# Output projection from rounded parts, with the gate on the result, more work buffers and another order of issue

## The chip, the core and the metric

The kernel runs on one core of one Trainium2 chip. A core has a matrix engine (TensorE, PE in the profile, with its weight loads listed as PEld), a vector engine (VectorE, DVE), an activation engine (ScalarE, ACT), a general engine (GpSimd, POOL) and an engine that here only issues transfers (SyncE, SP). Each takes its own instructions in the order in which they stand, and waits on semaphores for the others. Work data lie in an on-chip memory of 128 partitions (SBUF), matrix results in a second one (PSUM). Transfers are issued on the queue of SP or of POOL.

The metric is the device time of one execution in microseconds (us), as the median of several runs. Less is better.

## What is computed

One hybrid decoder layer for 1024 tokens of width 1024, float32 in and out. Normalised and modulated input goes through one projection into the inputs of two mixers: sparse attention with three branches (8 heads of 64), and a diagonal state-space model (S5). Each mixer's 512 columns are multiplied by a SiLU path, and both go through one output projection; its result is gated per column and added to the input:

```python
shift, scale, gate = jnp.split(silu(c) @ w_ada + b_ada, 3, axis=-1)
h = rms_norm(x, norm_g) * (1 + scale[:, None, :]) + shift[:, None, :]
proj = h @ w_in                                  # q, k/v of three branches, gate paths, S5 input
attn = nsa_attention(...) * silu(z_a)            # (1, 1024, 512)
ssm = glu(gelu(s5_mixer(u, ...))) * silu(z_s)    # (1, 1024, 512)
mix = jnp.concatenate([attn, ssm], axis=-1) @ w_out
return x + gate[:, None, :] * mix
```

The change concerns the last two lines above: the product with `w_out` (1024 x 1024), the gate, and the sum with x.

## The kernel before

Tokens are worked in 8 tiles of 128 (index i). The program is a list of some 500 named items. A table, `ORD`, gives the order in which the items are written; each item puts its instructions into the queues of the engines that it uses. What an engine does next is therefore set by `ORD` and by the way in which the items' instructions are merged per engine. A second table, `FLG`, says for single steps on which engine they run: "d" DVE, "p" POOL, "a" ACT, "t" a transfer that adds to what is there.

Stages, in the order in which they mainly run:

- Start. x is loaded in two halves (`xl_`), squared (`sq`), scaled (`xsc`) and transposed (`xb`). The modulation is computed from 24 chunks of `w_ada` (`ma`, `mb`, `mod`). `h_chunk` makes the modulated input h as two F32R tiles, a rounded part `hhi` and a rest `hlo`. The input projection (`kva`, `kvb`, `qa`, `qb`, `u`, `c_mms`) multiplies h with weights that are split in the same way (`split_w`: ACT copies the weight into an F32R tile, DVE or POOL subtracts that from the weight): rounded by rounded, rounded by rest, rest by rounded, three F32R matmuls into one sum. In the profile these are L325 to L327 and L346.
- S5 (`prep`, `tab`, `mats`, `scan`, `out`, four groups s). `mats` makes small matrices on PE (`pk`, `pw`) from tables that DVE and POOL prepare; `scan` makes `pvv` on PE, then a chain of ACT and DVE steps (`zw`, `z`), then PE takes `z` in the products `py` (L847, L848). Keys are normalised and rotated (`kpan`; the rotation writes `kr`) and transposed on PE (`kpat`, `pkt`, L474).
- Attention. For each of 8 tiles and 8 heads: `ha` (scores `S` on PE, L1147; the maximum on DVE, L1164; exp on ACT into `pp`, L1180), `hs`, `hb` (ACT scales into f16 `hl`, L1199), `hc` (DVE makes the f16 rest, L143; SP transposes `hl` into `PT` by transfer), `ub` (PE multiplies `PT` with the values V, L1240). Tiles run 0 to 3, then 7, 6, 5, 4. `z` pieces, items of the input projection, are spread between the heads.
- Output. `glu` writes the S5 half of the mix into `ps`. `wout(half, k)` loads 128 rows of `w_out` and multiplies them with the gate row, twice 128x512 on DVE. `ssm_out(i)` (`so`) multiplies the S5 half of tile i with weights of half 1 in float32 (L1041, `po<-wo,ps`) and DVE adds x from PSUM. `attn_trans(i)` (`at`) transposes the attention result and multiplies it with its SiLU path (`za`); `attn_out(i, n)` (`ao`) multiplies it with weights of half 0 (L1041, `po<-wo,za`) and `out_half` adds the S5 result and issues the store. The last tile, 4, does this in `last_out`, in two groups of heads.

One product here is one 128x128 block of the mix times one 128x512 block of `w_out`: 8 tiles x 2 halves of the columns x 4 blocks x 2 mixers are 128 products. A float32 product stands in the profile as two matmul records.

Work tiles come from pools of fixed slots: `w4` tiles of 4 KB per partition (`N4` = 16 slots), `w2` of 2 KB (`N2` = 12), `f2` of 2 KB in the late part (`F2` = 6). The default memory for the descriptors of POOL's transfers takes 16 KB of each partition.

Of the kernel before, what the change touches and what calls it, by code (L numbers as in the profile page):

```python
# [32 lines left out]
mats1 kpb0 kpb1 kpbn0 u1 u2 cU3 kpbn1 mod0 tab1 qaw0 xl1 u3 out0 prep2 scan1 cVC tab2 cmpk out1 qaw1 qaw2 cmpv kpbt0
xl2 mod1 mod2 mats2 qaw3 qa0 qaw4 hidk qaw5 cok kpbt1 qa1 mod3 qaw6 mod4 qa2 qa3 qaw7 prep3 mod5 tab3 mod6 qa4 qa5 qa6
qa7 qp0 qp1 qpn0 qpn1 qb0 tq qs0 hidv gw xl3 qs1 qw0 scan2 qr0 cz0 mats3 scan3 qb1 cov scalev qb2 qb3 cmpK qb4 gates
qt00 qb5 qb6 qb7 mod7 z0_0 modf cz2 cz1 z0_1 out2 qpb0 qpb1 qpbn0 g2 qt01 qpbn1 qsb1 z0_2 z0_3 ca0 z0_4 z0_5 z0_6 z1_0
z0_7 out3 kt ha00 ha01 qsb0 hs01 hb00 hc00 qw1 qr1 z1_1 z1_2 ct0 z1_3 ha02 ha03 hs03 hb01 hb02 z1_4 z1_5 cz3 ha04 hc01
hc02 z1_6 ha05 z1_7 hb03 hs05 hb04 hb05 yp00 z2_0 qt10 hc03 hc04 hc05 ha06 ha07 z2_1 z2_2 z2_3 z2_4 hs07 hb06 ha10 ca1
hb07 cz4 ha11 z2_5 ub00 qt11 ub01 hs11 hb10 hc06 hc07 z2_6 z2_7 hc10 ub02 qw2 ha12 yp01 ub03 hb11 qr2 ha13 ct1 z3_0
z3_1 z3_2 ub04 ub05 hs13 z3_3 z3_4 ha14 z3_5 ub06 ub07 cz5 hb12 hc11 hc12 ha15 hb13 z3_6 hc13 z3_7 hs15 hb14 qt20 z4_0  # L40
ha16 ha17 z4_1 ub10 ub11 hs17 hb15 hc14 hb16 ub12 yp02 z4_2 z4_3 ha20 ca2 hb17 hc15 hc16 qt21 z4_4 z4_5 cz6 z4_6 ub13
ha21 hs21 ha22 z4_7 yp03 hb20 hc17 ub14 yp10 ub15 hb21 z5_0 z5_1 z5_2 z5_3 qw3 qr3 ha23 hs23 hc20 hc21 hb22 ub16 cz7
# [1542 lines left out]
```

## Time and profile before

| | |
|---|---|
| median of 3 runs | 716.23 us (716.12 to 720.16) |
| profiled execution, its own time | 714.4 us |
| profiled execution, span of the core | 712.6 us |
| mean granted clock of TensorE in it | 0.983 |
| instructions in it | 12253 |

The profile is one execution on the chip. Its parts are the busy time of each engine, groups of equal instructions with mean duration and the idle time ahead of them, waits (who waited for whom), a timeline of single instructions, stretches of the span with the busy time of each engine in them, and the chain of work that ended last. A row of the timeline gives start, duration, engine, line, operation, what is written and from what, shape, count, and in square brackets how long the engine had been idle and what released it. Line numbers are those of the kernel before; in the changed kernel they are higher by 5 or more.

### The profile page before, as it was taken

The page shows a single profiled execution, that of the slowest core. Times are in us where ns is not written, and L with a number is a line of the kernel's source. Part 1 is how long each engine was busy: PE and PEld are TensorE (multiplying, and loading weights), DVE is VectorE, ACT ScalarE, POOL GpSimd, SP SyncE. Part 2 cuts the span into 40 slices and gives each one's busy share as a digit, 9 for nine tenths or more (in the row PEclk, how much of TensorE's full clock was granted, in tenths as well). Part 3 has the DMA queues.
Part 4 walks back from the last instruction along what each step waited for, and adds up shares of the span by engine and source line. Part 5 has one row for each costly group of instructions (what it writes and reads, how often), then busy time and mean ns, then how long its engine had stood idle before and what let it go on. Part 6 is the DMA issues. An engine that isn't in the chain of part 4 may idle for free. (4 is left out here: it accounts for less than half of the span.)

```text
span 712.6 us, 12253 instructions
## 1 busy us (share of the span) xinstructions
PE 640.2 (90%) x4534; PEld 469.4 (66%) x4534; DVE 541.3 (76%) x1077; ACT 359.2 (50%) x700; POOL 135.9 (19%) x152
## 2 busy tenths in 40 slices
PE   3399978599999999998998999998899899999997
PEld 1267767488788887886776776655566665665554
DVE  5989998678837889756686786988878786777561
ACT  4376205623551154446676775735575662755340
POOL 0150219247111020650201101120002011010000
PEclk9989998889999999999999999999999999999999
DMA  8963023046476723293556649769989795879674
GB/s 328 378 205 82 1 59 119 18 126 158 92 232 174 215 79 106 76 260 79 163 141 162 168 134 244 204 149 238 257 193 187 178 206 120 175 171 204 148 187 92
DMA packets 209470, 115.95 MB, mean 163 GB/s; under 512 B 159041, under 2 KB 188481, under 8 KB 209410
## 3 DMA queue, kind: packets, MB, share of 16 engines
q1 hardware_dynamic: 206146, 109.91, 60.3%
q0 software_dynamic: 3264, 5.26, 3.0%
q8 instruction: 36, 0.59, 0.4%
q14 instruction: 24, 0.20, 0.1%
HBM read 58.10 MB, written 18.61 MB: 108 GB/s over the span
## 5 line engine op out<-in xcount | busy, mean ns | idle before, releaser
L1180 ACT ACTIVATE pp<-S,st 128x640 f32<-128x640 f32 (+7 forms) x128 | 88.5, 697 | 75.1 <-DVE st L1164 53.8
L143 DVE SCALAR_TENSOR_TENSOR hl<-pp,st,hl 128x640 f16<-128x640 f32 (+7 forms) x128 | 94.9, 777 | 13.2 <-ACT hl L1199 12.7
L1199 ACT ACTIVATE hl<-pp,st 128x640 f16<-128x640 f32 (+7 forms) x128 | 85.7, 729 | 18.2 <-DVE hl L143 5.7
L346 PE MATMUL pcp<-hhi,wh 128*128 128x512 f32 x208 | 85.3, 410 | 2.8 <-DVE ql L143 2.1
L346 PE MATMUL pcp<-hhi,wl 128*128 128x512 f32 x208 | 82.9, 398 | 0.0
L346 PE MATMUL pcp<-hlo,wh 128*128 128x512 f32 x208 | 82.7, 398 | 0.0
L1164 DVE TENSOR_REDUCE st<-S 128x1 f32<-128x1024 f32 (+3 forms) x64 | 57.4, 917 | 12.2 <-PE S L1147 11.5
L325 PE MATMUL ptp<-wsp,hhi 128*128 128x512 f32 x128 | 52.3, 412 | 12.1 <-ACT hhi L291 12.1
L1147 PE MATMUL S<-kT,qh 128*128 128x512 f32 (+3 forms) x192 | 58.7, 363 | 1.7 <-ACT pp L1180 1.4
L1240 PEld LDWEIGHTS <-PT 128*128 128x128 f16 x1584 | 54.7, 98 | 7.4 <-issue 7.1
L1041 PE MATMUL po<-wo,za 128*128 128x512 f32 x128 | 58.6, 601 | 1.0 <-DVE za L143 0.6
L1240 PE MATMUL po<-V,PT 128*128 128x64 f16 x1584 | 58.7, 193 | 0.0
L1041 PE MATMUL po<-wo,ps 128*128 128x512 f32 x128 | 57.7, 599 | 0.4 <-DVE Sc L146 0.3
L1147 PE MATMUL S<-kT,ql 128*128 128x512 f32 (+3 forms) x192 | 53.6, 339 | 0.0
L327 PE MATMUL ptp<-wsp,hlo 128*128 128x512 f32 x128 | 51.7, 406 | 1.7 <-POOL hlo L146 1.3
L326 PE MATMUL ptp<-wsp,hhi 128*128 128x512 f32 x128 | 52.5, 410 | 0.1
L146 POOL TENSOR_TENSOR Sc<-Sc,lc 128x512 f32<-128x512 f32 x8 | 9.1, 1138 | 222.6 <-DVE lc L146 203.3
L1147 PEld LDWEIGHTS S<-kT,qh 128*128 128x128 f32 x192 | 32.6, 190 | 23.0 <-issue 18.1
L346 PEld LDWEIGHTS pcp<-hhi,wh 128*128 128x128 f32 x208 | 39.6, 190 | 11.3 <-issue 2.5
L346 PEld LDWEIGHTS pcp<-hlo,wh 128*128 128x128 f32 x208 | 39.2, 189 | 9.2
L346 PEld LDWEIGHTS pcp<-hhi,wl 128*128 128x128 f32 x208 | 39.3, 189 | 8.0
L1041 PEld LDWEIGHTS po<-wo,ps 128*128 128x128 f32 x128 | 23.4, 190 | 26.5 <-issue 24.4
(317 smaller groups left out, 1303.7 us busy)
## 6 DMA issues: line engine op xcount, KB each, us to landing
wada<-in_w_adaT_dram SPq DMA_DIRECT2D x24, 512.0 KB, 5.9
wr<-in_w_in_dram SPq DMA_DIRECT2D x14, 512.0 KB, 4.2
x<-in_x_dram SPq DMA_DIRECT2D x8, 512.0 KB, 5.8
wo<-in_w_out_dram SPq DMA_DIRECT2D x8, 512.0 KB, 5.3
xo<-in_x_dram SPq DMA_DIRECT2D x16, 256.0 KB, 4.1
out_dram<-ps SPq DMA_DIRECT2D x16, 256.0 KB, 2.4
wraw<-in_w_in_dram SPq DMA_DIRECT2D x15, 256.0 KB, 3.5
ud<-U SPq DMA_DIRECT2D x4, 512.0 KB, 3.1
```

What stands on the lines that cost most here:

```text
L143: dve.scalar_tensor_tensor(out=o, in0=a, scalar=s, in1=b, op0=o0, op1=o1, **kw)
L146: e.tensor_tensor(out=o, in0=a, in1=b, op=op)
L325: pe.matmul(p, H(k)[:, tsl], w[:, 0, :], start=k == 0, stop=False)
L326: pe.matmul(p, H(k)[:, tsl], w[:, 1, :], start=False, stop=False)
L327: pe.matmul(p, H(k, True)[:, tsl], w[:, 0, :], start=False, stop=k == 7)
L346: pe.matmul(p[:], w[:, k, :], H(k, l)[:, halves(half)], start=(k == 0 and w is hi and not l), stop=(k == 7 and l))
L1041: pe.matmul(p, a(k), M["wo", half, k][:, halves(n)], start=k == 0, stop=k == 3)
L1147: pe.matmul(R[:, c0:c1], w, x, start=bank not in opened, stop=False, skip_group_check=True)
L1164: dve.tensor_reduce(out=st[br], in_=us[br][0][:, :W], axis=AX.X, op=OP.max, negate=True)
L1180: act.activation(pp[:, :W], R[:, :W], AF.Exp, bias=st[br], accum_out=st4[:, 1, 2 * (h % 2) + br:2 * (h % 2) + br + 1])
L1199: act.activation(hl[:, :W], pp[:, :W], AF.Copy, scale=st[br])
L1240: pe.matmul(o, p, v, start=first, stop=end, skip_group_check=True)
```

## The change

- The weights of the output projection are loaded into a work tile (`wor`) and split into a rounded F32R tile and a rest, ACT copying and DVE subtracting (`wo..` is "d" throughout). The product with the gate row on the weights is gone.
- The mix of a tile is split as well (`parts`): ACT copies it into an F32R tile `oh`, DVE or POOL subtracts into `ol`. Of the 15 whole tiles, 9 subtractions are on POOL (`so0`, `so2`, `so7`, `at0` to `at3`, `at5`, `at6`) and 6 on DVE; the last tile's two halves are on DVE.
- A product becomes three F32R matmuls: 384 in place of 128 float32 products.
- The gate multiplies the result: `ssm_out` writes sum x 0.125 x gate into `ps` and then adds x, `out_half` writes sum x gate into a new tile `o` and then adds `ps`. That is two DVE steps of 128x512 where one stood. For tile 2 x is added by a transfer on POOL's queue.
- A weight needs two tiles now, so half 1 takes the slots that half 0 had. `wo0` therefore waits for all `so`, and `wo1` for all `glu`.
- The memory for descriptors is 2 KB, not 16; the 14 KB make three more `w4` slots and one more `w2`.
- `ORD` is another order; some `FLG` of the earlier stages move (three more parts of h by POOL transfer, two squares from DVE to ACT, one S5 step and one weight split from POOL to DVE, one weight split to POOL).

```diff
 ORD = """
-xl_0 sc1 sq1 sc0 sq2 sq3 sq0 rstd0 xsc0 xb10 ma0 ma5 mb0 xl_1 sq5 sq4 xb00 kvaw0 sq7 lb mg mc0 sq6 rstd1 h00 kva0 xsc1
+sc1 sc0 lb pu xl_0 sq0 sq2 sq1 sq3 ma7 mb4 ma0 rstd0 mb0 kvaw0 ma5 xl_1 xsc0 sq5 xb10 sq4 xb00 sq6 sq7 mg mc0 h00 mb2
...
-N4, N2, F2 = 16, 12, 6
+N4, N2, F2 = 19, 13, 6
+SCRATCH = 2048
...
     def wout(half, k):
-        w = p4([128, 1024], F32, "wo") if half else s4([128, 1024], F32, "wo", 0)
+        w = p4([128, 1024], F32R, "wo"), s4([128, 1024], F32R, "wo", 0)
         r0 = 512 * half + 128 * k
-        dma(w[:], t["w_out"][r0:r0 + 128, :], "o")
-        for n in range(2):
-            stt(w[:, halves(n)], w[:, halves(n)], 0.125 if half else 1.0, M["gate"][:, halves(n)], OP.mult, OP.mult)
+        on = FLG.get(f"wo{half}{k}", "d")
+        if on == "t":
+            fetch_w(w[0][:], w[1][:], t["w_out"][r0:r0 + 128, :])
+        else:
+            raw = w4([128, 1024], F32, "wor")
+            dma(raw[:], t["w_out"][r0:r0 + 128, :], "o")
+            split_w(w[0][:], w[1][:], raw[:], {"p": pool, "d": dve}[on])
         M["wo", half, k] = w
-    def outproj(p, a, half, n, ks=range(4)):
-        for k in ks:
-            pe.matmul(p, a(k), M["wo", half, k][:, halves(n)], start=k == 0, stop=k == 3)
+    def outproj(p, a, half, n, ks=range(4)):
+        for k in ks:
+            w = M["wo", half, k]
+            for m, (x, y) in enumerate(((0, 0), (0, 1), (1, 0))):
+                pe.matmul(p, a[x][:, k, :], w[y][:, halves(n)], start=k == 0 and m == 0, stop=k == 3 and m == 2)
+    def parts(a, tile_, on):
+        hi, lo = tile_([128, 4, 128], F32R, "oh"), tile_([128, 4, 128], F32R, "ol")
+        f = lambda x: x[:].rearrange("p a b -> p (a b)")
+        act.copy(f(hi), a)
+        tt(on, f(lo), a, f32(f(hi)), OP.subtract)
+        return hi, lo
     def ssm_out(i):
         ps = M["ps"]
-        sums = []
+        a = parts(ps[:, i, 0:512], f2, {"p": pool, "d": dve}[FLG.get(f"so{i}", "p")])
         for n in range(2):
-            xo = f2([128, 512], F32, "xo")
-            dma(xo[:], xr[:, i, halves(n)], "i")
             p = pmm("po")
-            outproj(p[:], lambda k: ps[:, i, 128 * k:128 * k + 128], 1, n)
-            sums.append((p, xo))
-        for n, (p, xo) in enumerate(sums):
-            tt(dve, ps[:, i, halves(n)], p[:], xo[:], OP.add)
+            outproj(p[:], a, 1, n)
+            stt(ps[:, i, halves(n)], p[:], 0.125, M["gate"][:, halves(n)], OP.mult, OP.mult)
+            on = FLG.get(f"xa{i}", "d")
+            if on != "t":
+                xo = f2([128, 512], F32, "xo")
+                dma(xo[:], xr[:, i, halves(n)], "i")
+                tt({"p": pool, "d": dve}[on], ps[:, i, halves(n)], ps[:, i, halves(n)], xo[:], OP.add)
+        if on == "t":
+            pool.dma_start(ps[:, i, :], xr[:, i, :], accum_op=OP.add)
...
     def out_half(i, n, p):
-        o = M["ps"][:, i, halves(n)]
-        tt(dve, o, p[:], o, OP.add)
-        dma(out.rearrange("(a p) d -> p a d", p=128)[:, i, halves(n)], o, "O")
+        r = M["ps"][:, i, halves(n)]
+        o = f2([128, 512], F32, "o")
+        tt(dve, o[:], p[:], M["gate"][:, halves(n)], OP.mult)
+        on = FLG.get(f"ao{i}{n}", "d")
+        if on == "t":
+            pool.dma_start(o[:], r, accum_op=OP.add)
+        else:
+            tt({"p": pool, "d": dve}[on], o[:], o[:], r, OP.add)
+        dma(out.rearrange("(a p) d -> p a d", p=128)[:, i, halves(n)], o[:], "O")
     def last_out(i, g):
...
+        hi, lo = LO["a"]
+        act.copy(hi[:, kk], za[:, kk])
+        tt(dve, lo[:, kk], za[:, kk], f32(hi[:, kk]), OP.subtract)
...
-            I(f"wo{h}{k}", "grow", *([f"wo{h}{k - 1}"] if k else []), *([] if h else glus))(lambda h=h, k=k: wout(h, k))
+            I(f"wo{h}{k}", "grow", *([f"wo{h}{k - 1}"] if k else []), *(glus if h else [f"so{i}" for i in range(NT)]))(lambda h=h, k=k: wout(h, k))
```

The other order at three places. First, PE's row at the end of the first projections (`ptp`), where the rotated keys are transposed (`pkt`); `pcp` are products of the input projection, `pk` and `pw` the small S5 matrices. Before:

```order
L325 MATMUL ptp<-wsp,hhi_92 128x512
L326 MATMUL ptp<-wsp,hhi_92 128x512
L327 MATMUL ptp<-wsp,hlo_94 128x512
L474 MATMUL pkt<-ident,kr 128x128 x8
L346 MATMUL pcp<-hhi_91,wh_322 128x512
L346 MATMUL pcp<-hhi_91,wl_323 128x512
```

and after (15 rows of `pk` stand between the last `ptp` and the first row here):

```order
L782 MATMUL pk<-s5CA,BD 48x112
L795 MATMUL pw<-ident,s5W 128x128 x4
L351 MATMUL pcp<-hhi_91,wh_318 128x512
L351 MATMUL pcp<-hhi_91,wl_319 128x512
L351 MATMUL pcp<-hlo_93,wh_318 128x512
L351 MATMUL pcp<-hhi_91,wh_318 128x512
L351 MATMUL pcp<-hhi_91,wl_319 128x512
L351 MATMUL pcp<-hlo_93,wh_318 128x512
L351 MATMUL pcp<-hhi_91,wh_318 128x512
L795 MATMUL pw<-ident,s5W 128x128 x4
L479 MATMUL pkt<-ident,kr 128x128 x4
```

The transposes of the keys moved behind the 16 products `pk`, both `pw` and 7 products `pcp`, and come in fours.

Second, PE's row at the first S5 result (`py`), further on. Before, `py` follows the second group's `pk` and `pw` directly:

```order
L775 MATMUL pk<-s5c,BD 48x16
L777 MATMUL pk<-s5CA,BD 48x112
L790 MATMUL pw<-ident,s5W 128x128 x8
L847 MATMUL py<-s5X,s5T 128x128
L848 MATMUL py<-z,s5CA 128x127
```

and after:

```order
L351 MATMUL pcp<-hlo_94,wh_1016 128x512
L351 MATMUL pcp<-hhi_92,wh_1016 128x512
L351 MATMUL pcp<-hhi_92,wl_1017 128x512
L351 MATMUL pcp<-hlo_94,wh_1016 128x512
L852 MATMUL py<-s5X,s5T 128x128
L853 MATMUL py<-z,s5CA 128x127
```

Between the second group's first `pw` and `py` stand 48 products `pcp` now, with the second `pw` and 8 transposes `pkt` among them (the last four products are shown).

Third, DVE's row where the last S5 products of the output end and the attention products begin (`hl` and `st` belong to the heads, `mc` and `Sc` to the compressed branch). Before, from a last sum with x to the first final sum:

```order
L146 TENSOR_TENSOR ps<-po,xo 128x512 x2
L1164 TENSOR_REDUCE st<-S 128x1 x2
L143 SCALAR_TENSOR_TENSOR za<-za,vsc,pat 128x512
L1188 RECIPROCAL st<-st 128x4
L143 SCALAR_TENSOR_TENSOR za<-za,vsc,pat 128x512
L146 TENSOR_TENSOR st<-st,gcol 128x4
L1164 TENSOR_REDUCE st<-S 128x1
L143 SCALAR_TENSOR_TENSOR hl<-pp,st,hl 128x768
L143 SCALAR_TENSOR_TENSOR hl<-pp,st,hl 128x640
L1164 TENSOR_REDUCE st<-S 128x1 x2
L146 TENSOR_TENSOR ps<-po,ps 128x512
```

and after, from the split of the weights of half 0 to the first final sum:

```order
L151 TENSOR_TENSOR wo<-wor,wo 128x1024
L1120 TENSOR_REDUCE mc<-pc_6793 128x8
L151 TENSOR_TENSOR wo<-wor,wo 128x1024
L155 TENSOR_SCALAR mc<-mc 128x8
L151 TENSOR_TENSOR Sc<-pc_6793,mc 128x512
L151 TENSOR_TENSOR wo<-wor,wo 128x1024 x2
L1125 TENSOR_REDUCE lc<-Sc 128x8
L148 SCALAR_TENSOR_TENSOR hl<-pp,st,hl 128x768
L148 SCALAR_TENSOR_TENSOR hl<-pp,st,hl 128x640
L155 TENSOR_SCALAR lc<-lc 128x8
L151 TENSOR_TENSOR o<-po,gate 128x512
```

The four subtractions of the weights, which had no counterpart here, moved between the last `so` and the first `ao`.

More of the change, by code (lines that the diff above doesn't have):

```diff
@@ L33 @@
[L33 to L42, printed above, removed]
@@ new lines @@
+h20 xb21 h30 kvaw3 xb11 h11 h21 xb31 kvaw6 xb40 h31 ma4 s5l mc4 h40 xb70 mc7 ll h70 xb50 u0m u1m ma6 u2m mc5 h50 kva0
+mc6 kva1 xb51 kva2 u3m xb61 xb60 h51 h61 xb71 h60 kva3 xb41 tb h41 kva4 kvaw7 h71 s5p u4m kva5 kva6 u5m kva7 u6m sw
+tabf kpa0 kpa1 cKC kpan0 kvb0 kvb1 kvb2 prep0 kvb3 kvb4 kvb5 u7m u0 cU2 kvb6 mats0 xl0 kpat0 tab0 prep1 scan0 kpan1 u1
+cU3 mats1 kpat1 xl1 kvb7 kpb0 tq kpb1 kpbn0 u2 qaw0 u3 mod0 mod1 out0 prep2 tab1 cVC kpbn1 scan1 out1 tab2 xl2 cmpk
+qaw1 cmpv kpbt0 qaw2 qa0 mod2 mod3 mod4 mats2 hidk qaw3 qaw4 qaw5 qa1 qa2 kpbt1 qa3 qa4 qa5 mod5 qaw6 qa6 mod6 qaw7
@@ new lines @@
+hb62 ub75 ha64 hc61 hc62 hb63 ha65 ub76 hs65 hb64 hb65 ha66 ha67 so4 ub77 ca5 ub60 ub61 hc63 hc64 so5 qt50 ha50 qt51
+ub62 hs67 hb66 hb67 hc65 qw4 qr4 ub63 so7 hc66 ha51 hs51 hc67 ub64 hb50 hb51 hc50 hc51 so6 ha52 ha53 ha54 ha55 ha56
+hs53 ub65 hb52 hb53 ub66 so3 wo00 wo01 wo02 wo03 ct5 hc52 qt41 at3 hc53 ub67 ub50 hs55 hb54 hb55 hc54 ha57 hs57 ca4
+ao30 hc55 hb56 hb57 ao31 ao00 ao01 qt40 at1 ha40 at2 ao10 ha41 hc56 hs41 hb40 hb41 hc57 hc40 ha42 ub51 ao11 ha43 ub52
+ao20 hs43 hb42 hb43 ct4 hc41 hc42 ao21 ub53 ub54 ha44 ha45 at7 ub55 ub56 ub57 ao70 hc43 hs45 hb44 hb45 ao71 ha46 ub40
@@ L56 @@
+at5 at6 ha47 hc44 ao50 ao51 ao61 hs47 hc45 hb46 hc46 hb47 ao60 ub41 ub42 ub43 hc47 ub44 ub45 ub46 ub47
 """.split()
@@ L1275, in attn_trans @@
         stt(zf, zf, vsc[:, 0:1], pt[:], OP.mult, OP.mult)
-        AT[i] = za
+        AT[i] = parts(zf, w2, {"p": pool, "d": dve}[FLG.get(f"at{i}", "p")])
     def attn_out(i, n):
         p = pmm("po")
-        outproj(p[:], lambda k: AT[i][:, k, :], 0, n)
+        outproj(p[:], AT[i], 0, n)
         out_half(i, n, p)
     def out_half(i, n, p):
-        o = M["ps"][:, i, halves(n)]
-        tt(dve, o, p[:], o, OP.add)
-        dma(out.rearrange("(a p) d -> p a d", p=128)[:, i, halves(n)], o, "O")
+        r = M["ps"][:, i, halves(n)]
[7 more added lines that the diff above has]
+        dma(out.rearrange("(a p) d -> p a d", p=128)[:, i, halves(n)], o[:], "O")
     LO = {}
@@ L1292, in last_out @@
         if g == 0:
-            za = LO["za"] = f2([128, 4, 128], F32, "za")
+            za = LO["za"] = w4([128, 4, 128], F32, "za")
             dma(za[:], zad[:, :, i * 128:(i + 1) * 128], "C")
+            LO["a"] = w4([128, 2, 4, 128], F32R, "oh")
+            LO["a"] = [LO["a"][:, n] for n in range(2)]
             LO["p"] = [pmm("po") for _ in range(2)]
@@ L1573 @@
     from concourse.bass_utils import run_bass_kernel_spmd as _run
-    nc = _bacc.Bacc("TRN2", target_bir_lowering=False, num_devices=1)
+    nc = _bacc.Bacc("TRN2", target_bir_lowering=False, num_devices=1, dynamic_dma_scratch_size=SCRATCH)
     arrays, args = {}, {}
```

47 lines of the change are left out of this document (25 added, 22 removed).

## The prediction

> **What bounds the kernel now.** I read the page's busy times first, then the same by stretches of the span, then the longest waits of PE in the timeline. The page:
>
> ```profile
> PE 640.2 (90%) x4534; PEld 469.4 (66%) x4534; DVE 541.3 (76%) x1077; ACT 359.2 (50%) x700; POOL 135.9 (19%) x152
> ```
>
> PE idles for 712.6 - 640.2 = 72.4 us. Where, and beside what, the stretches tell (columns: stretch, length, then busy time of PE, PEld, DVE, ACT, POOL, the granted clock, the share of the DMA engines, GB/s):
>
> ```profile
> 0.00:71.00 71.00, 44.39 (x180) 30.70 (x181) 59.73 (x187) 39.89 (x59) 14.54 (x16) 0.95 0.73 249
> 71.00:142.00 71.00, 55.52 (x292) 44.51 (x290) 60.37 (x175) 26.82 (x46) 29.33 (x30) 0.93 0.17 49
> 214.00:285.00 71.00, 69.91 (x400) 56.64 (x399) 61.50 (x119) 23.23 (x41) 6.81 (x6) 1.00 0.50 144
> 427.00:498.00 71.00, 67.31 (x543) 41.68 (x543) 60.74 (x88) 38.87 (x72) 12.24 (x8) 1.00 0.89 209
> 498.00:570.00 72.00, 65.64 (x665) 45.28 (x665) 58.81 (x83) 45.94 (x79) 4.72 (x4) 1.00 0.92 205
> 570.00:641.00 71.00, 69.03 (x601) 44.91 (x601) 52.63 (x82) 38.61 (x69) 7.62 (x6) 1.00 0.78 169
> 641.00:677.00 36.00, 36.00 (x232) 20.81 (x231) 23.16 (x34) 16.01 (x29) 0.00 (x0) 1.00 0.80 174
> 677.00:712.00 35.00, 29.36 (x327) 17.94 (x326) 13.16 (x20) 8.70 (x16) 0.00 (x0) 1.00 0.59 142
> ```
>
> Of the idle time 26.6 and 15.5 us lie in the first two rows, 42 of 72. From 427 us on, where the changed work lies, PE is busy for 67.31 + 65.64 + 69.03 + 36.00 + 29.36 = 267.3 of 285 us and idles for 17.7 (6%). DVE works 208.5 us there (73%), ACT 148.1. So from 142 us on PE is the bound: work taken from it shortens the span, unless DVE, which is given work, takes over.
>
> **The change part by part.**
>
> The products (A). Before, 256 float32 matmul records are 128 products. What three F32R matmuls take, the input projection shows, which multiplies in the same form; the first two rows are groups of the page (busy time, mean ns of one | idle ahead), the last two are stretches of L346 alone:
>
> ```profile
> L1041 PE MATMUL po<-wo,za 128*128 128x512 f32 x128 | 58.6, 601 | 1.0 <-DVE za L143 0.6
> L1041 PE MATMUL po<-wo,ps 128*128 128x512 f32 x128 | 57.7, 599 | 0.4 <-DVE Sc L146 0.3
> ...
> 285.00:356.00 71.00, 44.23 (x176) 32.00 (x175) 1.00 0.55 145
> 356.00:427.00 71.00, 46.13 (x186) 33.95 (x185) 1.00 0.59 149
> ```
>
> The mean of a record, 0.60 us, is not what it costs, since records overlap: 116.3 us of busy time over 128 products is 0.909 us each. The F32R form costs (44.23 + 46.13) / 362 = 0.2496 us a matmul, its own starts included, so 384 take 95.9 us. PE is given 116.3 - 95.9 = 20.4 us less. Both figures are at a granted clock of 1.00 and with a weight load for every matmul. I take -20.4 in full, as the stage is PE's.
>
> The Trainium skill, "FP8 and Floating Point Precision", section TensorE Precision Notes, says that true FP32 takes four passes through the array. As an estimate from it, three passes for four would give 116.3 / 4 = 29.1 us less; the rows say 20.4, and I go by the rows.
>
> The two waits of PE that the other order passes (B). The longest waits of PE after the start, with rows of the S5 matrices whose starts give their length:
>
> ```profile
> 109.60 1.97 PE L474 MATMUL pkt<-ident,kr 128*128 128x128 f32 x8 [6.73 <-POOL kr L146]
> 118.01 0.26 PE L775 MATMUL pk<-s5c,BD 128*48 128x16 f32 x2
> 120.39 0.66 PE L790 MATMUL pw<-ident,s5W 128*128 128x128 f32 x4
> 120.81 0.48 PE L346 MATMUL pcp<-hhi,wh 128*128 128x512 f32 x1
> 136.39 0.46 PE L847 MATMUL py<-s5X,s5T 128*128 128x128 f32 x2 [1.21 <-ACT s5B L791]
> 142.73 0.80 PE L848 MATMUL py<-z,s5CA 128*128 128x127 f32 x2 [5.88 <-DVE z L146]
> ```
>
> At the first place 16 `pk` (118.01 to 120.39: 2.4 us), two `pw` (0.42 each) and 7 products (7 x 0.25) now stand ahead of `pkt`: 5.0 of the 6.73 us are covered, if the S5 tables are ready in time; bounds 0 and -6.7. At the second 48 products, 12 us, cover 1.21 + 5.88 = 7.1; bounds 0 and -7.1. That work is taken from a later place where PE is the bound, so the waits are really gone: -12.1. The other order can open waits elsewhere; the trace of before can't show them. Bounds: 0, and the 13.8 us of these two, the largest that this program had. I take +3, near the low end, since the next longest wait of PE after 142 us is a short one (total, times, longest):
>
> ```profile
> PE pcp L346 <- DVE ql L143: 2.1, 1, 2.1
> ```
>
> The start. The changed order loads two small vectors earlier and the second half of x later; PE's row is nearly the same. Its waits there:
>
> ```profile
> 24.00 0.80 PE L325 MATMUL ptp<-wsp,hhi 128*128 128x512 f32 x1 [6.69 <-ACT hhi L291]
> 35.85 0.79 PE L325 MATMUL ptp<-wsp,hhi 128*128 128x512 f32 x1 [5.38 <-ACT hhi L291]
> ```
>
> Both end when modulated h arrives, behind loads and DVE's sums. DVE loses two squares of 1.2 us ahead of the second. I take 0; bounds -3 and +3, about that size.
>
> DVE, ACT and POOL in the output stage (C). Prices, as groups (min/median/max ns) and as page rows:
>
> ```profile
> L143 DVE SCALAR_TENSOR_TENSOR wo<-wo,gate x16: 677/680/693, 447.7 to 516.6; 128x512 f32<-128x512 f32 x16
> L146 DVE TENSOR_TENSOR ps<-po,xo x16: 679/680/693, 494.1 to 602.2; 128x512 f32<-128x512 f32 x16
> L146 DVE TENSOR_TENSOR wl<-wr,wh x13: 1206/1225/1832, 42.5 to 399.1; 128x1024 fp32r<-128x1024 f32 x13
> L146 DVE TENSOR_TENSOR kk<-kk,gains x8: 416/419/1496, 99.5 to 151.4; 128x256 f32<-128x256 f32 x8
> L203 ACT CAST wh<-wr 128x1024 fp32r<-128x1024 f32 x14 | 14.7, 1051 | 8.2 <-DMA wr<-in_w_in_dram 8.2
> L203 ACT CAST wsp<-wraw 128x512 fp32r<-128x512 f32 x15 | 8.8, 624 | 4.9 <-DVE wada L143 2.4 <-DMA wraw<-in_w_in_dram 2.4
> L146 POOL TENSOR_TENSOR hlc<-Sc,hlc 128x512 f16<-128x512 f32 x8 | 9.9, 1235 | 8.3 <-ACT hlc L1110 8.3
> ```
>
> DVE loses 16 gate steps on weights and 32 sums from PSUM, 48 x 0.68 = 32.6. It gets 32 gate steps from PSUM, 30 sums and 6 subtractions of 128x512, 68 x 0.68 = 46.2, 8 of 128x1024 at 1.225 = 9.8, and 2 of 128x256 at 0.42 = 0.8. Net +24.2. ACT gets 8 x 1.05 + 15 x 0.62 + 0.8 = 18.5, which leaves it at (148.1 + 18.5) / 265 = 63%: hidden in its idle time, at no cost. POOL gets 9 subtractions, 11 us, in a stage where it worked 24.6 of 285. They aren't free for DVE:
>
> ```profile
> 587.74 3.21 POOL L146 TENSOR_TENSOR qr<-ropeb 128x512 f32<-128x512 f32 x2 [7.43 <-DVE ropeb L146]
> 588.26 3.38 DVE L143 SCALAR_TENSOR_TENSOR hl<-pp,st,hl 128x768 f16<-128x768 f32 x2
> 591.96 1.81 DVE L143 SCALAR_TENSOR_TENSOR hl<-pp,st,hl 128x768 f16<-128x768 f32 x2 [0.32 <-ACT hl L1199]
> ```
>
> The same pair takes DVE 3.38 us beside two POOL steps and 1.81 alone: 0.8 a step, so 9 steps make 7. DVE then has 208.5 + 24.2 + 7 = 240 us to do beside 267.3 - 20.4 = 247 of PE. That is about 90% of the stage, and PE waits more at such a load: in the three stretches shown from 142 us on with DVE above 80% it idled 1.5% (214), 5% (427) and 9% (498). I take the last, which is this stage's own: 247 / 0.912 = 271, against 285 - 20.4 = 264.6 with A alone: +6. Bounds: 0, and DVE as the bound at the share it reached at 214, 87%: 240 / 0.87 = 276, +11.
>
> Here a rule speaks against the change. The Trainium skill, "SBUF — State Buffer", section Who interferes with whom, says that a DVE instruction with two SBUF inputs contends with a POOL instruction that reads SBUF, and that one with at most one SBUF input does not. The row agrees (`pp` and `hl` are both in SBUF). By the rule each POOL step may block DVE for its whole length, 9 x 1.235 = 11 us for my 7, and the 30 new sums, both inputs in SBUF, are exposed where the old sums from PSUM were not; as an estimate from it the sum would be up to 4 us longer.
>
> Handover from `so` to `ao` (D). The weights of half 0 reuse slots that the last `so` still reads, so 4 copies (1.05) and 4 subtractions (1.225), some 6 us, start only then. On DVE the heads' `hl`, `mc` and `Sc` stand between them and are delayed by up to 4.9. On PE three blocks of PV, two of scores and small transposes stand between the last `so` and the first `ao`; the chain of waits has such blocks:
>
> ```profile
> 651.67 1.56 PE S L1147 x11
> ...
> 656.72 1.05 PE po L1240 x36
> ```
>
> Two blocks of scores and three of PV are 3.1 + 3.2, with the transposes 7 to 8 us: cover for the 6. I take +1; bounds 0 and +6.
>
> The end (E). The chain closes with `za`, the last products and one sum, then the store:
>
> ```profile
> 705.24 3.71 PE po L1041 x8
> 708.98 0.69 DVE ps L146
> ```
>
> Now a copy of 128x256 (about 0.4) goes ahead, 12 matmuls take 3.0, then come two DVE steps, 1.37: 4.8 against 4.4, +0.4.
>
> POOL's transfers and the rest. With less descriptor memory an issue may have to wait for an earlier landing, and three more parts of h and x of tile 2 now come by POOL's queue. The burst of issues ahead of the first heads, and landings (KB, us):
>
> ```profile
> 299.37 3.79 POOL L1458 DMA_DIRECT2D kT<-kTd  x7
> ...
> hlo<-hf POOLq DMA_DIRECT2D x2, 256.0 KB, 4.5
> kT<-kTd POOLq DMA_DIRECT2D x8, 256.0 KB, 4.6
> ```
>
> I take 0, since products of other blocks of h, or of the input projection, stand ready beside them; bounds 0 and one landing, 4.6. The other engine moves of early steps leave DVE within 0.3 us of before (7 steps of 0.68 to 1.2 us come, 6 go) and take work from POOL, which has room: 0. The extra slots: 0. Weights, x and result move the same bytes on SP's queue: 0.
>
> **Sum.** -20.4 - 12.1 + 3 + 6 + 1 + 0.4 = -22.1. Against the execution's own time, 714.4, that is 692.3. The median stands 1.8 above that execution, which gives 694.
>
> **The rivals.**
>
> B1, better: no new waits, and the stage keeps its 6%. -20.4 x 1.06 - 12.1 + 0.4 = -33: 681 + 2 = 683. For it: DVE at 87% cost PE 1.5% at 214 us. Against: the heads need DVE twice per head, at 498 us that cost 9%.
>
> B2, DVE becomes the bound of the output stage: C is 11, D 6, new waits 6. -20.4 - 12.1 + 6 + 11 + 6 + 0.4 = -9: 705 + 2 = 707. For it: 240 against 247 us. Against: at 677 us DVE has much room, and its new sums lie there in part.
>
> B3, the other order gives nothing early (13.8 us of new waits) and DVE bounds: -20.4 - 12.1 + 13.8 + 11 + 1 + 0.4 = -6, to +2 with D in full and the start's 3: 710 to 718, no change. It says that the change doesn't do what it says outside PE.
>
> B4, slower. DVE's row is in order, and each `hl` and each maximum stands behind gate steps and sums that wait for PE's products, so that both wait for each other. With B + D + E at -7.7, slower by 1% needs a stage of 285 + 7.7 + 7.2 = 300 us: DVE below 240 / 300 = 80% of it. At 76%, 316 us: 714.4 - 7.7 + 31 + 1.8 = 740. For it: DVE ran at 74% in the row at 570 us. Against: there it had no more to do; where it had, it reached 82 to 87%.
>
> **Chances.** Forecast 694 (own range 688 to 701): 0.48. B1 0.18, B2 0.18, B3 0.11, B4 0.05. A measurement of this kernel can tell about 1% from no change: 709 and 723 are the bounds. Faster: the first three and a little of B3, 0.86; same 0.10; slower 0.04. The range takes in B1 and B2: 681 to 708.
>
> **What would show it.** A: `po<-wo,oh` and `po<-wo,ol` together near 96 us of busy time, 384 records. B: no wait of PE above 2 us between 95 and 150 us, and more busy time of PE in 71 to 142. C: DVE's busy time near 573, PE's idle time from 427 us on near 24. D: `wo` of half 0 split within 8 us, PE not waiting for `wo`. E: two DVE steps at the end, less than 5 us after the last `za`. The forecast is wrong if PE's records don't shrink, if DVE's share in the stage stays below 80% while PE waits for it, or if new waits of several us appear in the first 300 us.

## The result, and the profile after

The changed kernel takes 694.52 us in the median of four runs (691.0 to 697.8), the kernel before 716.17 (715.28 to 720.16). The ratio is 0.9686, with a 95% interval of 0.9627 to 0.9746: by the ratio 22.5 us less, between 18 and 27. The forecast was 694. The profiled execution is the longest of the four, 697.8 us with a span of 695.9, 16.7 less than that of before.

The page of the changed kernel, busy times, and its stretches (the columns are those of the prediction):

```profile
PE 628.0 (90%) x4662; PEld 497.7 (72%) x4662; DVE 567.8 (82%) x1106; ACT 378.3 (54%) x732; POOL 147.1 (21%) x159
...
0.00:71.00 71.00, 42.18 (x160) 28.84 (x161) 56.24 (x160) 43.67 (x65) 18.38 (x19) 0.95 0.77 264
71.00:142.00 71.00, 68.03 (x350) 54.82 (x349) 64.22 (x200) 30.50 (x50) 22.20 (x25) 0.98 0.22 64
142.00:427.00 285.00, 273.66 (x1737) 224.25 (x1736) 218.42 (x424) 143.89 (x341) 71.10 (x89) 0.98 0.56 151
427.00:720.00 293.00, 244.15 (x2421) 189.75 (x2419) 228.90 (x325) 160.27 (x281) 35.42 (x26) 0.97 0.77 172
```

The span ends at 695.9, so the last row is a stretch of 268.9 us. PE idles there for 268.9 - 244.15 = 24.7 us, against 18.3 before (285.6 - 267.33). Ahead of it PE idles for 28.8 + 3.0 + 11.3 = 43.1 us, against 54.1 (72.4 in all, less 18.3). The second row holds most of that: 3.0 us of idle time for 15.5. So idle time shrinks by 11.0 early and grows by 6.4 late. DVE has 26.5 us more to do in all, ACT 19.1, POOL 11.2.

The products of the changed line, first their groups (min/median/max ns), then their busy time in the stage, then the same of the float32 products of the kernel before:

```profile
L1053 PE MATMUL po<-wo,oh x264: 387/395/795, 486.9 to 690.9; 128*128 128x512 f32 x132
L1053 PE MATMUL po<-wo,ol x120: 388/395/628, 487.5 to 676.9; 128*128 128x512 f32 x120
...
427.00:720.00 293.00, 100.42 (x384) 0.97 0.77 172
...
427.00:720.00 293.00, 116.35 (x256) 1.00 0.80 180
```

384 records and 100.4 us where 256 took 116.35 before. The median record is 395 ns; the twelve that start between 607.8 and 612.7 us, in a stretch at half clock, take 628, one of them 795. The clock in this stage (0.97 in the row, 1.00 before) is what the forecast had no term for. It is lowered where PE has waited:

```profile
125.10 3.46 PE L824 MATMUL pvv<-s5X,s5B 128*128 128x128 f32 x16 [2.39 <-DMA s5X<-ud]
188.33 0.80 PE L853 MATMUL py<-z,s5CA 128*128 128x127 f32 x2 [6.15 <-DVE z L151]
470.88 0.27 PE L1170 MATMUL S<-dmask,identb 128*128 128x128 bf16 x1 [3.38 <-ACT pp L1203]
490.44 0.22 PE L1170 MATMUL S<-dmask,identb 128*128 128x128 bf16 x1 [2.33 <-ACT pp L1203]
606.07 0.50 PE L1053 MATMUL po<-wo,oh 128*128 128x512 f32 x1 [2.13 <-DVE wo L151]
...
460.00:480.00 20.00, 16.62 (x124) 0.83 0.86 203
480.00:500.00 20.00, 17.30 (x283) 0.91 1.04 205
600.00:620.00 20.00, 16.05 (x136) 0.83 0.91 239
```

The last three rows are windows of 20 us: length, busy time of PE, granted clock. Each of the three waits from 470 us on is followed by a stretch at half clock: 0.83 of 20 us is 6.8 us at 0.5, 0.91 is 3.4. The wait for `kr` (6.73 us before) is gone. That for `z` is not: before it stood at 142.73 with 5.88, now it stands at the next S5 block with 6.15, where it was 1.31. The wait for `s5X` is new.

### The profile page after: what moved, and what is told of

Its sections match the earlier page's. It is cut to its first block, busy times and chain, and to the rows that moved or that the text cites. A ratio compares the mean times of both kernels' runs of the same rounds, so it can differ in the third digit from the quotient of the medians.

```text
span 695.9 us, 12617 instructions
## 1 busy us (share of the span) xinstructions
PE 628.0 (90%) x4662; PEld 497.7 (72%) x4662; DVE 567.8 (82%) x1106; ACT 378.3 (54%) x732; POOL 147.1 (21%) x159
## 4 chain that ended last, share of the span: by engine, by line
PE 39%; DVE 24%; issue 5%; ACT 4%; DMA 1%; POOL 1%; SPq 0%; DVEq 0%; ACTq 0%; POOLq 0%
PE pcp L351 9%; PE po L1053 8%; PE S L1170 7%; DVE hl L148 5%; DVE st L1187 3%; PE pglu L1015 3%; PE po L1263 3%; PE ptp L332 2%; PE ptp L331 1%; DVE ps L151 1%; PE ptp L330 1%; DVE o L151 1%; ACT pp L1203 1%; DVE z L151 1%; PE pg L530 1%
## 5 line engine op out<-in xcount | busy, mean ns | idle before, releaser
L148 DVE SCALAR_TENSOR_TENSOR hl<-pp,st,hl 128x640 f16<-128x640 f32 (+7 forms) x128 | 100.6, 818 | 4.7 <-ACT hl L1222 4.5
L1053 PE MATMUL po<-wo,oh 128*128 128x512 f32 x264 | 86.5, 412 | 4.3 <-DVE wo L151 3.1
L1053 PEld LDWEIGHTS po<-wo,oh 128*128 128x128 f32 x264 | 49.5, 194 | 15.7 <-DVE wo L151 4.2
L330 PE MATMUL ptp<-wsp,hhi 128*128 128x512 f32 x128 | 53.5, 420 | 5.0 <-ACT hhi L296 3.1
L1170 PE MATMUL S<-kT,ql 128*128 128x512 f32 (+3 forms) x192 | 56.0, 349 | 0.2 <-DVE ql L148 0.2
L332 PE MATMUL ptp<-wsp,hlo 128*128 128x512 f32 x128 | 53.4, 418 | 1.9 <-POOL hlo L151 1.9
L331 PE MATMUL ptp<-wsp,hhi 128*128 128x512 f32 x128 | 53.0, 414 | 0.9 <-DVE wsp L151 0.9
L151 POOL TENSOR_TENSOR qr<-ropeb 128x512 f32<-128x512 f32 x16 | 23.5, 1491 | 121.5 <-DVE ropeb L151 69.9
L1053 PE MATMUL po<-wo,ol 128*128 128x512 f32 x120 | 48.3, 406 | 0.8 <-DVE ol L151 0.8
```

Source lines behind the costliest of these rows:

```text
L148: dve.scalar_tensor_tensor(out=o, in0=a, scalar=s, in1=b, op0=o0, op1=o1, **kw)
L151: e.tensor_tensor(out=o, in0=a, in1=b, op=op)
L330: pe.matmul(p, H(k)[:, tsl], w[:, 0, :], start=k == 0, stop=False)
L331: pe.matmul(p, H(k)[:, tsl], w[:, 1, :], start=False, stop=False)
L332: pe.matmul(p, H(k, True)[:, tsl], w[:, 0, :], start=False, stop=k == 7)
L1053: pe.matmul(p, a[x][:, k, :], w[y][:, halves(n)], start=k == 0 and m == 0, stop=k == 3 and m == 2)
```

## The experiments

Twelve kernels, each beside runs of the kernel before on the same chip. "Order" is the list of items, with the engine table that belongs to it. "Early" is the part of the list up to its 436th item, which holds the same items in both kernels, just ahead of the opening of the late pools; "late" is the rest. The edits shown are against the changed kernel, that of `before_slots19` against the kernel before.

| kernel | early order | late order | projection | slots | ratio to before | interval |
|---|---|---|---|---|---|---|
| changed | new | new | three products | 19, 13 | 0.9686 | 0.9627 to 0.9746 |
| parts_only | old | old | three products | 16, 12 | 1.0472 | 1.0399 to 1.0544 |
| parts_slots19 | old | old | three products | 19, 13 | 1.0400 | 1.0358 to 1.0442 |
| before_slots19 | old | old | float32 | 19, 13 | 1.0066 | 1.0040 to 1.0093 |
| order_only | new | new | float32 | 19, 13 | 0.9946 | 0.9906 to 0.9986 |
| early_only | new | old | float32 | 19, 13 | 0.9808 | 0.9759 to 0.9856 |
| late_only16 | old | new | three products | 16, 12 | 0.9951 | 0.9920 to 0.9982 |
| slots16 | new | new | three products | 16, 12 | 1.0303 | 1.0247 to 1.0360 |
| scratch_only | new | new | three products | 16, 12 | 1.0331 | 1.0276 to 1.0386 |
| xa_t | new | new | three products | 19, 13 | 0.9796 | 0.9749 to 0.9842 |
| fill | new | new | three products | 19, 13 | 0.9688 | 0.9630 to 0.9745 |
| no_gate | new | new | three products, less a gate | 19, 13 | 0.9667 | 0.9626 to 0.9708 |
| moved | new | new, three items moved | three products | 19, 13 | 0.9650 | 0.9610 to 0.9690 |

### The products in the old order

```diff
-N4, N2, F2 = 19, 13, 6
-SCRATCH = 2048
+N4, N2, F2 = 16, 12, 6
+SCRATCH = 16384
```

Beside these lines the list of items and the engine table are those of before, with `wo10` to `wo13` behind `glu13` and `wo00` to `wo03` behind `so3`.

> The projection as three products with the gate on the result, in the order, the slots, the engine table and the descriptor memory of before; only the weights of half 1 are moved behind the last GLU block and those of half 0 behind the last SSM tile, as their slots need it, and x comes by plain transfers. By the terms of the prediction (A -20.4, C +6, D +1, E +0.4) it is 13 us faster than before, 703. If the gain needs the other order (the old one puts the new DVE steps where PE then waits for them), it is 710 or more, with PE's idle time from 427 us on above 30 us. If the products give their 20 us and DVE costs nothing, 696.

750.1 us, 4.7% slower than before. The theory that the gain needs the other order holds (710 or more, idle time above 30 us), by far more than I had thought. Its waits of PE from 427 us on (total, times, longest):

```profile
PE S L1161 <- ACT pp L1194: 15.0, 13, 3.9
PE po L1254 <- DMA PT<-hl: 13.6, 13, 3.1
PE pat L1287 <- DMA A<-ad: 6.3, 2, 3.2
PE po L1044 <- ACT oh L1050: 4.1, 3, 3.2
...
427.00:800.00 373.00, 264.87 (x2483) 204.32 (x2481) 236.95 (x333) 162.69 (x286) 36.47 (x26) 0.93 0.62 140
```

The span is 742.4, the stage 315.4 us. PE idles for 50.5 of them, and DVE, at 237, is only 75% busy. Neither is full: the scores wait for softmaxes, the PV products for the transposed `hl`, the products for their parts. I read these as steps that stand behind others in the rows of DVE and ACT or in SP's queue; the waits fit that, but no run moves single steps of this kernel. It is the mechanism of B4, with DVE's share below the 80% that the prediction named as its sign. The clock of the stage is 0.93.

> The three products in the order of before, with 19 and 13 slots and the smaller descriptor memory. That kernel took 750 with 16 and 12. If the slots are what it lacked, 700 to 710. If the order is what it lacked (the new steps of DVE, ScalarE and the weights' loads stand where TensorE then waits for them), it stays above 735.

The same kernel without the four changed lines above, so with the slots and descriptor memory of the changed kernel: 743.45, still 4.0% slower. What it lacks is the order.

### The order without the products

```diff
-            outproj(p[:], a, 1, n)
-            stt(ps[:, i, halves(n)], p[:], 0.125, M["gate"][:, halves(n)], OP.mult, OP.mult)
...
+            outproj(p[:], lambda k: ps[:, i, 128 * k:128 * k + 128], 1, n)
+            sums.append((p, xo))
```

> The projection in float32 with the gate in the weights, as before, in the order, slots, engine table and descriptor memory of the changed kernel. By term B (-12.1 + 3) it is 707, with the wait for kr and its half-clock stretch gone. If what the order gains early it pays back in new waits and lowered clock, it is 714 to 718. If the order carries most of the change, below 702.

All functions of the projection as before, of which the diff shows two lines, all else as in the changed kernel: 710.65, 0.5% faster, about 4 us for the 9 of the term, between the first two theories. In the profiled execution the last product of the input projection starts at 424.3 us (425.0 in the changed kernel, 433.4 before), so it enters the output stage with the lead, and from 427 us on PE idles for 25.7 us where it idled for 18.3 before: the lead is lost there, in a late order that was written for the three products. So the order was also taken apart: here the late part of the list is the old one, with the dependencies that it had for the weights.

```diff
-            I(f"wo{h}{k}", "grow", *([f"wo{h}{k - 1}"] if k else []), *(glus if h else [f"so{i}" for i in range(NT)]))(lambda h=h, k=k: wout(h, k))
+            I(f"wo{h}{k}", "grow", *([f"wo{h}{k - 1}"] if k else []), *([] if h else glus))(lambda h=h, k=k: wout(h, k))
...
```

> The float32 projection of before, with the changed kernel's order, engine table, slots and descriptor memory ahead of the opening of the late pools, and the order of before behind it. It is term B by itself (-12.1 + 3): 707 if the 8 to 12 us by which the changed kernel enters the output stage earlier reach the end. If the output stage takes the lead back (waits of TensorE for others than itself), 711 to 715.

703.65, 1.9% faster: 13.8 us, between 10 and 17. This is term B alone (the early order with its engine table and slots), and the lead does reach the end. Its stretches:

```profile
0.00:71.00 71.00, 43.38 (x167) 30.01 (x168) 57.96 (x172) 45.38 (x67) 19.11 (x22) 0.93 0.77 264
71.00:142.00 71.00, 68.73 (x368) 55.41 (x368) 66.00 (x194) 31.31 (x49) 23.57 (x24) 1.00 0.24 68
142.00:427.00 285.00, 273.14 (x1764) 222.60 (x1764) 216.66 (x420) 145.40 (x346) 70.51 (x89) 0.98 0.57 155
427.00:720.00 293.00, 253.59 (x2239) 161.40 (x2237) 200.28 (x292) 139.12 (x246) 23.36 (x16) 1.00 0.75 167
```

PE idles for 2.3 us between 71 and 142, where it idled for 15.5 before. In the late stage it idles for 272.7 - 253.59 = 19.1 us (18.3 before): nothing is lost again.

> The three products with the changed kernel's order from the opening of the late pools on (item 437 of the list), and the order, engine table, slots (16 and 12) and descriptor memory of before ahead of that. If the products need only their own order behind that point, and the slots are needed by the early order alone (where the kernel with 16 slots lost 37 of its 43 us), it is 694 to 702: some 18 us faster than before, without what the early order gives. If the late order needs the slots too, 715 or more.

The other half, the late order with the products, on the old early part with its 16 and 12 slots: 713.35, 0.5% faster, at the upper end of what lay between the two theories. The late order turns the 29 to 34 us that the products lose in the old one into a gain, but of 3.5 us only. What it lacks against the changed kernel the traces divide: the last product of the input projection starts 10.7 us later (435.7 against 425.0 us), and from there to the end it takes 277.9 us for 270.9, 7.0 more. The first is the missing early order; whether the second is the missing slots, no kernel tells.

### The slots and the descriptor memory

```diff
-N4, N2, F2 = 19, 13, 6
-SCRATCH = 2048
+N4, N2, F2 = 16, 12, 6
+SCRATCH = 16384
```

> The changed kernel with the slots (16 and 12) and the descriptor memory (16384) of before. By the prediction both are worth nothing: 694, within 3 us. If the three more slots let transfers start that the new order needs, it is 700 or more, with longer waits of PE for wl, wh or hlo before 142 us. If the smaller descriptor memory costs POOL's transfers time, it is faster than 691.

737.27, 3.0% slower than before, by the ratios some 44 us slower than the changed kernel (39.4 between the two profiled executions). The prediction had these slots at 0. Where the time goes shows on SP's queue (start, length of the issues, what). First the changed kernel, then this one, and below them its longest waits of PE between 142 and 427 us:

```profile
203.87 1.30 SPq L140 DMA_DIRECT2D wada<-in_w_adaT_dram  x2
209.39 5.44 SPq L140 DMA_DIRECT2D s5T<-Kt  x8
214.93 1.96 SPq L140 DMA_DIRECT2D wraw<-in_w_in_dram  x4
...
209.56 0.82 SPq L140 DMA_DIRECT2D wada<-in_w_adaT_dram  x2
216.93 5.18 SPq L140 DMA_DIRECT2D s5T<-Kt  x8
222.15 2.01 SPq L140 DMA_DIRECT2D wraw<-in_w_in_dram  x4
...
PE ptp L330 <- ACT wsp L208: 6.9, 1, 6.9
PE S L1170 <- ACT pp L1203: 6.2, 2, 3.9
```

The weights `wraw` are issued at 222.15 instead of 214.93, by a chain that starts at a slot. The load of `wada` at 209.56 has waited 4.1 us until DVE had read an earlier `wada` tile and freed its slot; in the changed kernel the two loads are issued at 203.87. DVE's step on the late tile runs from 215.47 to 216.69, and `Kt` stands behind it in DVE's row (216.62; 209.05 in the changed kernel). The load of `s5T` from `Kt` waits for that, and `wraw` stands behind this load in SP's queue. PE then waits 6.9 us for the parts of `wraw`. Waits of this kind repeat: the last product of the input projection starts at 462.1 us here and at 425.0 in the changed kernel, so 37 of the 39 us lie ahead of the output stage.

```diff
-N4, N2, F2 = 19, 13, 6
+N4, N2, F2 = 16, 12, 6
```

> The changed kernel with the slots of before (16 and 12) and its own smaller descriptor memory (2048). It splits the 45 us by which 16 and 12 slots with 16384 were slower than the changed kernel. If the slots are what its order needs, it is 737 again. If the larger descriptor memory was what cost the time, 694. In between, each has the share that this shows.

738.41: the same within the intervals. The descriptor memory makes no difference that shows here, as predicted; the slots are the loss.

And the kernel before with the lines of the changed kernel:

```diff
-N4, N2, F2 = 16, 12, 6
+N4, N2, F2 = 19, 13, 6
-    nc = _bacc.Bacc("TRN2", target_bir_lowering=False, num_devices=1)
+    nc = _bacc.Bacc("TRN2", target_bir_lowering=False, num_devices=1, dynamic_dma_scratch_size=2048)
```

> The kernel before with 19 and 13 slots and the smaller descriptor memory, nothing else. If slots are worth something by themselves, it is 5 us or more below the kernel before. If its order was made for 16 and 12 slots, it is within 4 us of it, which is what the prediction took for the slots (0).

719.58, 0.7% slower. In the old order more slots, with the smaller descriptor memory that makes room for them, are no gain, even a small loss; which of the two costs it is not shown. A slot has no price of its own: it has one in an order that is written for it.

### DVE's load in the output stage

```diff
-        tt(dve, o[:], p[:], M["gate"][:, halves(n)], OP.mult)
...
-            tt({"p": pool, "d": dve}[on], o[:], o[:], r, OP.add)
+        tt(dve, o[:], p[:], r, OP.add)
```

> The changed kernel with the gate left out of the attention part: out = product + SSM part, one step of DVE in place of two (the SSM part keeps its gate). 16 steps of 0.68 us leave DVE, 11 us, and nothing else changes. By term C, DVE's load is what makes TensorE idle more in the output stage: its idle time from 427 us on falls from 25 towards 18 and the time by 4 to 7, to 687 to 690. If DVE's load costs nothing there and its place in the order alone does, 693 to 696.

This kernel leaves the gate out of the attention part, so it doesn't compute the layer; it only prices the 16 steps. 693.21, by the ratios 1.4 us less than the changed kernel, uncertain by 5: the time alone can't tell this from the 4 to 7 us that term C would give. The stretches can. The 16 steps stand at 614 us and later in the changed kernel, so here is its output stage in two parts, then that of this kernel:

```profile
427.00:612.00 185.00, 169.25 (x1647) 128.74 (x1646) 167.73 (x230) 123.27 (x213) 26.57 (x20) 0.96 0.85 187
612.00:720.00 108.00, 74.91 (x776) 61.01 (x774) 61.17 (x96) 37.00 (x69) 8.86 (x6) 0.98 0.64 147
...
427.00:612.00 185.00, 169.12 (x1668) 129.45 (x1665) 167.81 (x234) 123.23 (x212) 25.84 (x20) 0.96 0.84 185
612.00:720.00 108.00, 70.92 (x748) 58.29 (x744) 49.27 (x75) 34.84 (x64) 8.03 (x6) 1.00 0.63 145
```

From 612 us to the end (695.9 and 691.8) DVE has 49.3 us to do in place of 61.2, and PE idles for 79.8 - 70.92 = 8.9 us, where it was 83.9 - 74.91 = 9.0. Twelve us less on DVE take no idle time from PE there. Ahead of 612, where PE idles for 15.8 of its 24.7 us and DVE is busy for 91% of the time, DVE's load is the same in both kernels: this kernel says nothing on that part.

```diff
...
-xa0="d", xa1="d", xa2="t", xa3="d", xa4="d", xa5="d", xa6="d", xa7="d"
+xa0="t", xa1="t", xa2="t", xa3="t", xa4="t", xa5="t", xa6="t", xa7="t"
...
```

> The changed kernel with x added to the SSM part by POOL's accumulating transfers for all eight tiles and not for tile 2 alone: 14 sums of 0.68 us leave DVE in the output stage, 9.5 us, and seven transfers of 512 KB come to POOL's queue. If DVE's load costs TensorE its waits there (term C), TensorE idles some 4 us less from 427 us on and the kernel is 688 to 691. If DVE's load is not what it waits for, 694. If the transfers come late, or take POOL time that its subtractions need, 697 or more.

701.09, 1% slower than the changed kernel by the ratios. DVE is relieved here too, ahead of 612 us, but one new wait decides, the third row, with SP's queue above it:

```profile
590.69 3.34 SPq L130 DMA_DIRECT2D wor<-in_w_out_dram  x4
594.09 8.73 SPq L1226 DMA_TRANSPOSE PT<-hl  x2
...
PE po L1253 <- DMA PT<-hl: 11.8, 2, 10.0
```

The loads of the four weights of half 0 stand ahead of two transposes, and these are issued only at 594.09 and take 8.7 us. In the changed kernel the four loads stand ahead of the same two transposes (597.08 and 601.51). What differs is PE's row: there the products with this `PT` start at 615.15, behind the first products of half 0; here they stand ahead of them, and PE waits 10 us. The list of items is the same, but the way in which their instructions are merged is not. So this kernel doesn't price DVE's load, and the load ahead of 612 us stays without a clean test.

### The waits and the clock

```diff
+    def fill(n):
+        p = pmm("fill")
+        for _ in range(n):
+            pe.matmul(p[:], kT[:, 0, 0:128], kT[:, 0, 0:512], start=True, stop=True)
...
```

> The changed kernel with matrix products on TensorE whose result nobody reads: 12 before the scores of head 3 of tile 7 (where it waited 3.4 us at 470), 8 before those of head 5, and 10 before the first products of tile 3's attention part (where it waited 2.1 us at 606). If a wait of 2 us or more lowers the granted clock, and the half clock costs what it takes from the products behind it, the stretches of half clock at 470 and 606 (6.8 us each) are gone and the kernel is up to 6 us faster, 688 to 692. If TensorE at half clock hides behind the engines that it waited for, the clock rises but the time stays, 694. If the clock doesn't follow the waits, the stretches stay and it is 694 to 698.

693.2, ratio 0.9688: no difference from the changed kernel that these runs show. The filling stood where it should at the first and third place; at the second the wait stayed (2.59 us), as that work was issued elsewhere. The other way is to put work that is needed there (pieces of the list, before and after the edit):

```diff
-hc37 hc70 at0 ha73 hs73 glu13 wo10
+hc37 hc70 glu13 at0 ha73 hs73 wo10
...
-at3 hc53 ub67 ub50 hs55 hb54 hb55 hc54 ha57 hs57 ca4 ao30
+at3 hc53 hs55 hb54 hb55 hc54 ha57 hs57 ca4 ub67 ub50 ao30
```

> The changed kernel with three items moved: the last GLU block ahead of the turn of tile 0 and of head 3 of tile 7, and the PV products of two heads ahead of the first attention products, so that work of its own stands where TensorE waited 3.4 us at 470 and 2.1 at 606. If these waits and their half clock cost what they take, 688 to 691, better than both kernels. If TensorE only waits somewhere else for the same late steps of DVE, 693 to 697.

692.34, ratio 0.9650: the lowest of all, but its interval covers the changed kernel's 0.9686, so that it is better than that one is not shown. The windows of the two kernels, first `fill`, then `moved`, to be read against the three rows of the first section:

```profile
460.00:480.00 20.00, 19.43 (x256) 1.00 1.00 202
480.00:500.00 20.00, 17.40 (x153) 0.91 0.76 186
600.00:620.00 20.00, 18.46 (x165) 1.00 0.92 227
...
460.00:480.00 20.00, 18.41 (x234) 1.00 0.98 232
480.00:500.00 20.00, 16.12 (x195) 1.00 0.95 195
600.00:620.00 20.00, 17.14 (x170) 1.00 1.12 262
```

The clock follows the waits: where they are filled or moved, it is 1.00. By the ratios the time follows by 0 us and by 2.6, each uncertain by 5 to 6, so a gain of a few us could hide there. The traces point to one: from the start of the last product of the input projection (425.0, 421.4 and 425.2 us) to the end, the changed kernel takes 270.9 us, `fill` 267.6 and `moved` 266.9, each in one execution. That is 3.3 and 4.0 us less, for 13.6 and 17 us of half clock taken away. In `moved` PE idles from 427 us on for 24.7 us, as in the changed kernel, in shorter pieces.

## Why the prediction was right, and where it wasn't

The time came out within 1 us, and that is in part luck, as two of its terms were off in opposite directions. The kernels divide the 22.5 us into 13.8 for the early order (`early_only`) and 8.7 for the products with their late order, by the difference of the two ratios, 0.9808 and 0.9686 (uncertain by 5 to 6 us). The prediction had 9.1 and 13.0.

The two profiled executions lie 16.7 us apart, for the 22.1 of the sum: that of before (714.4 us) is below the four runs of its kernel, that of after the longest of its four. They divide so: the products take 15.9 us less of PE, its idle time ahead of 427 us is 11.0 less and from there on 6.4 more, and PE's other work takes 3.7 more. The last had no term; the lowered clock would make such a loss, but no run separates it.

**A (-20.4): a little too large.** PE's busy time for the products fell by 15.9 us, and by 17.9 in `moved`, which has hardly a lowered clock there (98.45 us). A matmul costs 98.45 / 384 = 0.256 us and not the 0.2496 of the input projection; the rest of the shortfall goes with the lowered clock. The estimate of 29.1 from the four passes of the Trainium skill ("FP8 and Floating Point Precision", TensorE Precision Notes) is not borne out.

```profile
427.00:720.00 293.00, 98.45 (x384) 0.99 0.78 172
```

**B (-12.1 + 3): right in kind, a little too small.** The wait for `kr` is gone in full. The second of the two waits was passed, but a wait for `z` of the same size opened at the next S5 block, and the sign "no wait above 2 us between 95 and 150" failed by one, 2.39 us for `s5X`. The stretches give 11.0 us of PE's idle time ahead of 427 for the 9.1, and `early_only`'s 12.3 (54.1 against 27.6, 2.3 and 285 - 273.14 = 11.9 in its stretches). In the traces the last product of the input projection starts at 431.0 to 435.7 us in the three kernels with the old early part and 16 slots, and at 420.8 to 425.2 in the seven with the new early part and 19: on average 10.3 us earlier. So B lies between about 10 and the 13.8 that `early_only`'s time gives.

**The start (0): right.** PE first waits 14.9 us for x, 6 us more than before, and has caught up by 71 us but for 2.2: idle for 28.8 against 26.6. In that is a new wait of 2.2 us for a part of h that POOL's queue brings, a term taken as 0 with a bound of 4.6.

**C (+6) and D (+1): the sum held, the mechanism of C didn't.** PE's idle time in the stage grew by 6.4 us, 7 were forecast, and DVE's busy time came out at 567.8 for 573. But C laid the idle time on DVE at 90% load, and the load doesn't explain where it grew. The stretch from the first product of half 1 to the last, before, after, and in `xa_t`:

```profile
485.30:601.60 116.30, 108.22 (x962) 70.08 (x961) 92.58 (x131) 67.04 (x112) 10.14 (x8) 1.00 0.91 202
486.90:593.10 106.20, 98.37 (x951) 80.02 (x948) 98.28 (x140) 69.06 (x118) 14.05 (x12) 0.98 0.91 188
483.50:588.60 105.10, 99.72 (x962) 81.23 (x958) 91.04 (x131) 70.40 (x122) 18.62 (x18) 0.98 0.97 183
```

DVE's share rises from 80 to 93%, and PE idles for 7.8 us where it idled for 8.1. From the first product of half 0 to the end PE idles for 11.7 us where it idled for 7.1; that is most of the growth, in a stretch in which DVE is busy for 75%, and `no_gate` takes DVE's load there down to 66% with PE idle for 11.4. Against this reading stands that `xa_t`, with DVE at 87%, idles for 5.4 us in the stretch above; its rows changed too, so that a share of C there is not excluded. The waits from 427 us on tell what grew:

```profile
PE S L1170 <- ACT pp L1203: 11.0, 13, 3.4
PE po L1053 <- DVE wo L151: 3.1, 3, 2.1
PE pc L1114 <- ACT qc L1111: 1.7, 3, 1.2
PE po L1053 <- ACT oh L1337: 1.2, 2, 1.0
PE po L1053 <- DVE ol L151: 0.8, 1, 0.8
```

Rows two, four and five are products that wait for their own parts, 5.1 us; before, products waited 1.1 us for their operands `za` and `Sc`. The scores wait 2.3 us more for the softmax (8.7 before). D saw the handover of the weights (predicted: split within 8 us, PE not waiting) and priced it at 1: the four weights are split from 602.2 to 610.8, and PE waits 2.7 of the 3.1 us for them. The step that failed is C's reading of the stretch at 498: that PE idled 9% there beside a DVE at 82% was taken for an effect of the load. What the runs show in its place are waits for single steps, of which the parts are the larger share; that these come from the place of the steps in their rows is how I read it, and no run moves them alone. The price of a POOL step beside DVE was sound: over all DVE steps from 427 us on, the time above the median of the same step without POOL beside it is 5 to 6 us before and 10 to 12 after, by how the steps are grouped, so 0.6 to 0.8 us for each of the nine new POOL steps where 0.8 was taken.

**E (+0.4): right.** The end, from the last `za` (687.79) to the last sum (692.79), is 5.0 us for the predicted 4.8:

```profile
687.81 0.41 ACT oh L1337
...
688.27 3.08 PE po L1053 x12
...
691.37 0.70 DVE o L151
...
692.10 0.69 DVE o L151
```

**The extra slots (0): wrong as a price.** Without them the changed order is 3.0% slower than before. The term was right for the sum only because order and slots came together.

**Not in the sum: the clock.** Half of PE's busy time at half clock is 17 us in the profiled execution after, 7 before (its stretches in the trace, each with PE's busy time in it). That execution is also 5.5 us above the forecast's 692.3. The executions of the changed kernel from 691.0 to 697.8 us go with granted clocks from 0.978 down to 0.973. By the traces of `fill` and `moved`, 3 to 4 us of it in the output stage can be had back.

**B4 (0.05): the rival that the experiments made real.** Products given to an order that was not made for them cost 4 to 5%, by waits of several engines for each other with none of them full.

## What to carry to other kernels

Work taken from the bound engine counts only if what it is exchanged for (here splits, gates and sums on three other engines) doesn't hold that engine up: by the order and the slots around them the same three products cost 34 us, or gained 3.5 or 9. Price a step that a row has to do by who waits for it and not by the share of time for which its engine is busy; leaving a step out, as in `no_gate`, shows which of the two it is, for the stretch in which the step stands and no other. Slots and order are one choice: the new slots in the old order were a small loss, and the whole new order with the old slots a large one.
